# MLP first matrix on one Trainium2 core: PSUM banks of a pair laid out anew, first operands split during the output projection

## The chip, the cores and the metric

The kernel runs on one core of one Trainium2 chip. The metric is the time of one execution in microseconds (us) on the device; the engines are TensorE (PE, with its weight loads as PEld), VectorE (DVE), ScalarE (ACT), GpSimd (POOL) and SyncE (SP), whose queue issues the DMAs.

## The reference, cut to what matters

One decoder block over 1024 tokens of width 1024: a normed input projection, two mixers (a gated linear recurrence and sparse attention), a gated merge, an output projection with residual, and then the part that this case is about:

```python
h = h + merged @ w_out[l]
hn = rmsnorm(h, norm2_g[l])
h = h + jnp.square(jax.nn.relu(hn @ w_ff1[l])) @ w_ff2[l]
return rmsnorm(h, final_g)
```

Everything is float32. `w_ff1` is 1024 x 4096, `w_ff2` 4096 x 1024.

## The kernel before

Each float32 matrix product is made from three matmuls on operands that are split into a high and a low part (high x high, high x low, low x high). A split is one cast on ScalarE (high) and one subtraction on VectorE (low).

**The last stages.** The merge and the output projection run for two halves of the tokens (`th` 0 and 1, four tiles of 128 tokens each). The projection has, for each half of the columns (`dh`) and each tile `j`, 24 matmuls into a PSUM tile `po`, an addition on VectorE into the residual `hx` (L1375), and for the last half (`th` 1, `dh` 1) the second norm of tile `j` from the generator `norm2` (`next(n21)` twice): a square on ScalarE (L248), two small instructions on GpSimd (L249, L250), the scaled row on VectorE (`hn`, L1122), and then four sums and differences of the token blocks, on VectorE (L1134, L1136) and GpSimd (L1135, L1137).

**The first matrix of the MLP** is a Strassen-Winograd product: 7 products instead of 8 for each block of 256 output columns, called a pair here; there are `NP` = 16 pairs. `FORDER` is the order of the products in a pair: P1, P6, P7, P2, P5, P4, P3. Pairs 0 and 1 are interleaved at the start: P1 of both, P2 of both, then the rest of pair 0 and of pair 1. A product is 12 matmuls of 128x512 with stationary weights `w1op` and moving token blocks `xoh`, `xol`. The token blocks A11 and A12 are ready early; S1, S2, S3, S4 and A22 are made by `turn` after the first six products (`TURNS`): 16 transposes each through four PSUM tiles `pt`, each emptied by a cast (L1113) and a subtraction (L1114).

**Weights.** `f1_load` brings the two halves of a pair's weights (`w1r`); `f1_sums` makes the four weight differences T1 to T4 with four subtractions on GpSimd (L1174, tile `w1t`); `f1_prep` splits one product's weights into a slot of the ring `w1op` (five slots; cast L1185, subtraction L1186). P1, P2 and P3 take the raw blocks B11, B21, B22; the other products take T1 to T4. `ahead(s)` keeps the splits four steps ahead of the products (`AHEAD`). Before the first product the kernel calls `f1_sums(0)`, `f1_sums(1)` and `ahead(0)`; later pairs call `f1_sums(p + 1)` from `f1_prep`.

**PSUM.** There are two kinds of PSUM tiles: `psA`, two of them, each of two banks, and `psB`, four of them, each of one bank (also used by `po` and `pt`). A pair needs four banks: `a` takes P1 and then P2 on top, `c` takes P6, `d` takes P7 and then P4, `e` takes P5 and then P3. Before, `a` and `c` are the halves of one `psA` tile, and `d` and `e` are a `psB` tile each:

```python
pa = psA("f1a")
PB[p] = {"a": pa[:, :512], "c": pa[:, 512:], "d": psB("f1d"), "e": psB("f1e")}
```

After P1 ScalarE copies bank `a` to `p1` (L1225). After P6 VectorE adds `c` and `p1` to `u2` (L1217); after P7 it adds `d` and `u2` to `u3`; after P5 `e` and `u3`; after P4 `d` and `u2`; after P3 `e` and `u2`. Relu, square and the sums of the results follow on ScalarE, VectorE and GpSimd, and the results go to DRAM (`u_d`). The second matrix (`g_mm`, tiles `gA` of kind `psA` and `gB` of kind `psB`) reads them back.

The kernel is written with a tile framework, which puts in the semaphore waits and decides, from the order of the program and its own idea of what is ready, the order of instructions on each engine. So an engine's order in the trace is not always the program's.

Of the kernel before, what the change touches and what calls it, by code (L numbers as in the profile page):

```python
# [54 lines left out]
def tile_hybrid_block(ctx, tc, x, positions, norm1_g, w_in, lb_param, hgrn_norm_g, pe_k, pe_v,  # L55
# [15 lines left out]
    def psA(name="psA"):  # L71
        return ps.tile([128, 1024], F32, name=name, tag="A", bufs=2)

    def psB(name="psB"):
        return ps.tile([128, 512], F32, name=name, tag="B", bufs=4)
# [48 lines left out]
    class Stream:  # L124
# [5 lines left out]
        def add(self, srcs, shape):  # L130
            self.specs.append((srcs if isinstance(srcs, list) else [srcs], shape))
# [35 lines left out]
    def w_cols(w, c0, n, k0=0, k=KT):  # L167
        return w[k0 * 128:(k0 + k) * 128, c0:c0 + n].rearrange("(a p) c -> p a c", p=128)
# [420 lines left out]
    for t in range(NT):  # L589
        p = psB("pp")  # L590
# [557 lines left out]
    NP = FF // 256  # L1148
    FORDER = ("P1", "P6", "P7", "P2", "P5", "P4", "P3")
    FX = {"P1": "A11", "P2": "A12", "P3": "S4", "P4": "A22", "P5": "S1", "P6": "S2", "P7": "S3"}  # L1150
    FW = {"P1": "B11", "P2": "B21", "P3": "B22", "P4": "T4", "P5": "T1", "P6": "T2", "P7": "T3"}
    W1R, W1S, FOP, PB = {}, {}, {}, {}
# [4 lines left out]
    def ring(key, n, i, dt=F32):  # L1157
        r = RING.setdefault(key, {})
        if i % n not in r:
            r[i % n] = s4(dt, name=key)  # L1160
        return r[i % n]

    def f1_load(p):
        W1R[p] = []
        for q in range(2):
            r = ring("w1r", 4, 2 * p + q).rearrange("p (a c) -> p a c", a=4)
            nc.sync.dma_start(r, w_cols(w_ff1[0], p * 256, 256, k0=4 * q, k=4))
            W1R[p].append(r)

    def f1_sums(p):  # L1170
        b11, b12 = W1R[p][0][:, :, :128], W1R[p][0][:, :, 128:]
        b21, b22 = W1R[p][1][:, :, :128], W1R[p][1][:, :, 128:]
        ta, tb = [ring("w1t", 4, 2 * p + q).rearrange("p (x a c) -> p x a c", x=2, a=4) for q in range(2)]
        sub = lambda o, x_, y_: nc.gpsimd.tensor_tensor(o, x_, y_, op=OP.subtract)  # L1174
        sub(ta[:, 0], b12, b11)
        sub(ta[:, 1], b22, ta[:, 0])
        sub(tb[:, 0], b22, b12)
        sub(tb[:, 1], b21, ta[:, 1])
        W1S[p] = {"B11": b11, "B21": b21, "B22": b22, "T1": ta[:, 0], "T2": ta[:, 1], "T3": tb[:, 0],
                  "T4": tb[:, 1]}  # L1180

    def split2(src, op, shape):

        h, l = [op[:, x_ * 512:(x_ + 1) * 512].rearrange("p (a c) -> p a c", a=shape) for x_ in range(2)]
        nc.scalar.copy(h, src)  # L1185
        nc.vector.tensor_tensor(l, src, fb(h), op=OP.subtract)  # L1186
        return h, l
# [1 line left out]
    n_op = [0]  # L1189

    def f1_prep(p, nm):
        if nm == FORDER[4 if p == 1 else 3] and 0 < p < NP - 1:
            f1_sums(p + 1)
        FOP[p, nm] = split2(W1S[p][FW[nm]], ring("w1op", 5, n_op[0], F32R), 4)
        n_op[0] += 1
        if nm == FORDER[-1]:
            del W1S[p], W1R[p]
            if p + 2 < NP:
                f1_load(p + 2)
# [2 lines left out]

    def f1_prod(p, nm):
        if nm == "P1":
            pa = psA("f1a")
            PB[p] = {"a": pa[:, :512], "c": pa[:, 512:], "d": psB("f1d"), "e": psB("f1e")}
        bank = {"P1": "a", "P2": "a", "P6": "c", "P7": "d", "P4": "d", "P5": "e", "P3": "e"}[nm]
        dst, first = PB[p][bank], nm in ("P1", "P6", "P7", "P5")
        h, l = FOP.pop((p, nm))
        xh, xl = XO[FX[nm]]  # L1210
        for kt in range(4):
            for i, (w_, x_) in enumerate(((h, xh), (h, xl), (l, xh))):
                nc.tensor.matmul(dst, w_[:, kt, :], x_.kt(kt), start=first and kt == 0 and i == 0,  # L1213
                                 stop=kt == 3 and i == 2, skip_group_check=True)
        post = UP.setdefault(p, {})
        ps_ = PB[p]
        add = lambda o, a, b: nc.vector.tensor_tensor(o, a, b, op=OP.add)  # L1217

        def sq(o, eng):
            nc.scalar.activation(o, o, AF.Relu)  # L1220
            eng.tensor_tensor(o, o, o, op=OP.mult)

        if nm == "P1":
            post["p1"] = mlp.tile([128, 512], F32, name="p1", tag="p1", bufs=2)
            nc.scalar.copy(post["p1"], ps_["a"])  # L1225
        elif nm == "P6":
            post["u2"] = mlp.tile([128, 512], F32, name="u2", tag="u2", bufs=2)
            add(post["u2"], ps_["c"], post["p1"])
        elif nm == "P7":
            post["u3"] = mlp.tile([128, 512], F32, name="u3", tag="u3", bufs=2)  # L1230
            add(post["u3"], ps_["d"], post["u2"])
        elif nm == "P2":
            ua = post["ua"] = ring("ua", 2, p).rearrange("p (x c) -> p x c", x=2)
            nc.scalar.activation(ua[:, 0], ps_["a"], AF.Relu)
            nc.gpsimd.tensor_tensor(ua[:, 0], ua[:, 0], ua[:, 0], op=OP.mult)
        elif nm == "P5":
            ua = post["ua"]
            add(ua[:, 1], ps_["e"], post["u3"])
            sq(ua[:, 1], nc.vector)
            nc.sync.dma_start(u_d[p][0:2].rearrange("x p c -> p x c"), ua)  # L1240
        elif nm == "P4":
            ua = post["ua"]
            ut = post["ut"] = ring("ut", 2, p).rearrange("p (x c) -> p x c", x=2)
            ub = post["ub"] = ring("ub", 2, p).rearrange("p (x c) -> p x c", x=2)
            add(ut[:, 0], ps_["d"], post["u2"])
            sq(ut[:, 0], nc.vector)
            nc.gpsimd.tensor_tensor(ub[:, 0], ua[:, 0], ua[:, 1], op=OP.add)
            nc.gpsimd.tensor_tensor(ub[:, 1], ut[:, 0], ua[:, 1], op=OP.add)
            nc.sync.dma_start(u_d[p][2:4].rearrange("x p c -> p x c"), ub)
        else:  # L1250
            ua, ut = post["ua"], post["ut"]
            add(ut[:, 1], ps_["e"], post["u2"])
            sq(ut[:, 1], nc.gpsimd)
            uc = ring("uc", 1, 0)[:, (p % 2) * 512:(p % 2) * 512 + 512]
            nc.vector.tensor_tensor(ut[:, 0], ut[:, 0], ua[:, 0], op=OP.subtract)
            add(uc, ua[:, 0], ut[:, 1])
            nc.vector.tensor_tensor(ut[:, 1], ut[:, 1], ua[:, 1], op=OP.subtract)
            nc.sync.dma_start(u_d[p][4], uc)
            nc.sync.dma_start(u_d[p][5:7].rearrange("x p c -> p x c"), ut)
            del UP[p], PB[p]  # L1260
# [74 lines left out]
    def ahead(s):  # L1335
        while n_load[0] < min(len(seq), s + LOADS + 1):
            g_load(*seq[n_load[0]][1:])
            n_load[0] += 1
        while n_prep[0] < min(len(seq), s + AHEAD + 1):
            k, a, b = seq[n_prep[0]]  # L1340
            (f1_prep if k == "f" else g_prep)(a, b)
            n_prep[0] += 1

    g2b = load_row(norm2_g)
    for th in range(2):
        if th == 0:
            drain(zb.pop(0))
        else:
            for _ in merge(1, 0.0):
                pump(1300)  # L1350
        hs_ = []
        for j in range(4):
            t = th * 4 + j
            hx = s4(name="hx")
            nc.sync.dma_start(hx, x2[t * 128:(t + 1) * 128, :])
            hs_.append(hx)
        for dh in range(2):
            ws = [W.get() for _ in range(4)]
            if th == 1 and dh == 0:
                drain(n2)  # L1360
            if th == 1 and dh == 1:
                n21 = norm2(1, hs_)
                f1_load(0)
                f1_load(1)
            for j in range(4):
                p = psB("po")
                sl = slice(j * 128, (j + 1) * 128)
                for kt in range(KT):
                    w = ws[kt // 2]
                    mh, ml = M[th][kt // 4][0][:, kt % 4, sl], M[th][kt // 4][1][:, kt % 4, sl]  # L1370
                    mm3(p, (mh, ml), (w[0][:, kt % 2, :], w[1][:, kt % 2, :]), kt == 0, kt == KT - 1)
                    if kt == 3:
                        pump(2600)
                hv = hs_[j][:, dh * 512:(dh + 1) * 512]
                nc.vector.tensor_tensor(hv, hv, p, op=OP.add)  # L1375
                if th == 1 and dh == 1:
                    next(n21)
                    next(n21)
                pump(2600)
            del ws  # L1380
        del M[th]
        if th == 0:
            n2 = spawn(norm2(0, hs_))
        else:
            f1_sums(0)
            f1_sums(1)
            ahead(0)
            hs_ = None
    yb = None
# [4 lines left out]
    for s, (k, a, b) in enumerate(seq):  # L1394
# [6 lines left out]
        i, p = a, b  # L1401
# [48 lines left out]
```

## Time and profile before

| | |
|---|---|
| median of 3 runs | 1675.06 us (1674.51 to 1677.39) |
| profiled execution, its own time | 1676.41 us |
| span of the profile | 1674.6 us |
| PE busy | 1612.9 us (96%), 8342 matmuls |
| DVE, ACT, POOL busy | 1041.9 us (62%), 738.7 us (44%), 584.2 us (35%) |
| TensorE clock granted, mean | 0.988 |
| output projection, last matmul starts | 992.74 us |
| MLP first matrix, first and last matmul start | 1000.02 and 1361.44 us |

The span is the profiler's view from the first to the last instruction; the execution's own time is 1.8 us longer. Times in the rows are microseconds from the span's start. A matmul's row lasts 0.39 us in the trace, but matmuls are pipelined: the distance between starts is what one costs. In a timeline row a pair of square brackets holds the idle time before the instruction on its engine and what ended it.

### The profile page before, as it was taken

How to read it: one execution, taken by the hardware profiler on the slowest of the kernel's cores; microseconds unless marked ns; L12 is line 12 of the kernel's file. 1: busy time of each engine (PE TensorE's matmuls, PEld its weight loads, DVE VectorE, ACT ScalarE, POOL GpSimd, SP SyncE). 2: the span in 40 equal slices, each digit the busy share in tenths (PEclk: the TensorE clock that was granted, in tenths of full speed). 3: DMA queues.
4: the chain of work that ended last, by engine and by line, in shares of the span. 5: the costliest groups of instructions: out<-in, count | busy, mean ns of one | idle time of the engine just before them, and what ended most of it. 6: DMA issues, size and time to landing. Idle time of an engine off the chain costs nothing. (4 is left out here: it accounts for less than half of the span.)

```text
span 1674.6 us, 22913 instructions
## 1 busy us (share of the span) xinstructions
PE 1612.9 (96%) x8342; PEld 1346.1 (80%) x8342; DVE 1041.9 (62%) x1612; ACT 738.7 (44%) x1410; POOL 584.2 (35%) x583
## 2 busy tenths in 40 slices
PE   8999999999999999999999988999999999999998
PEld 7899887889887887788788767777777788888886
DVE  5463454123555568888874728666566686887765
ACT  5433333321664457777753314333333355334442
POOL 2121221110124263443412134555555321565552
PEclk9999999999999999999999998999999999999999
DMA  5210111232433000000075711443344489889853
GB/s 184 70 51 14 40 37 51 73 106 80 137 126 117 14 1 1 2 1 1 14 264 196 244 50 51 151 139 134 130 138 138 140 279 359 290 308 338 301 176 107
DMA packets 145395, 211.67 MB, mean 126 GB/s; under 512 B 11601, under 2 KB 72193, under 8 KB 145282
## 3 DMA queue, kind: packets, MB, share of 16 engines
q1 hardware_dynamic: 145282, 210.21, 37.4%
q8 instruction: 66, 1.08, 0.3%
q14 instruction: 47, 0.39, 0.1%
HBM read 164.03 MB, written 46.14 MB: 126 GB/s over the span
## 5 line engine op out<-in xcount | busy, mean ns | idle before, releaser
L1302 POOL TENSOR_TENSOR gr<-gw 128x512 f32<-128x512 f32 x80 | 125.7, 1583 | 133.7 <-DVE gu L1186 50.8
L1213 PE MATMUL f1a<-xoh,w1op 128*128 128x512 f32 x384 | 135.7, 417 | 33.2 <-ACT p L1225 24.2
L155 POOL TENSOR_TENSOR wlo<-wraw,whi 128x1024 fp32r<-128x1024 f32 (+1 forms) x28 | 67.4, 2408 | 274.8 <-ACT whi L152 270.4
L242 PE MATMUL gT<-xh,whi 128*128 128x512 f32 x384 | 152.7, 398 | 0.0
L244 PE MATMUL gT<-xh,wlo 128*128 128x512 f32 x384 | 150.3, 391 | 0.0
L243 PE MATMUL gT<-xl,whi 128*128 128x512 f32 x384 | 150.1, 391 | 0.0
L919 POOL TENSOR_SCALAR P<-P,den,gat 128x640 f32<-128x640 f32 (+7 forms) x128 | 99.6, 793 | 120.5 <-DVE den L915 61.4
L155 DVE TENSOR_TENSOR wlo<-wraw,whi 128x1024 fp32r<-128x1024 f32 (+2 forms) x59 | 80.8, 1377 | 94.5 <-ACT whi L152 89.8
L1186 DVE TENSOR_TENSOR gu<-gr,gu 128x512 fp32r<-128x512 f32 x112 | 101.5, 906 | 46.7 <-ACT gu L1185 46.5
L1185 ACT CAST gu<-gr 128x512 fp32r<-128x512 f32 x112 | 69.5, 620 | 133.5 <-DVE gx L1186 105.8
L1213 PEld LDWEIGHTS f1a<-xoh,w1op 128*128 128x128 f32 x384 | 77.2, 201 | 56.7 <-ACT p L1225 30.1
L937 DVE TENSOR_TENSOR pth<-pT,pth 128x512 fp32r<-128x512 f32 (+1 forms) x148 | 98.7, 682 | 21.3 <-ACT pth L936 19.9
L1186 DVE TENSOR_TENSOR gx<-gr,gx 128x512 fp32r<-128x512 f32 x112 | 109.2, 975 | 3.9 <-ACT gx L1185 3.8
L910 ACT ACTIVATE P<-sc,den 128x640 f32<-128x640 f32 (+7 forms) x128 | 89.6, 704 | 44.0 <-DVE den L901 39.2
L894 PE MATMUL sc<-kS,qS 128*128 128x512 f32 (+3 forms) x384 | 96.7, 361 | 0.6 <-ACT P L910 0.5
L1045 PE MATMUL oT<-pth,vS 128*128 128x512 f32 x264 | 96.5, 440 | 0.0
L936 ACT CAST pth<-pT 128x512 fp32r<-128x512 f32 (+1 forms) x148 | 84.9, 587 | 23.9 <-PE pT L934 21.6
L901 DVE TENSOR_REDUCE den<-sc 128x1 f32<-128x640 f32 (+7 forms) x96 | 84.5, 883 | 16.7 <-PE sc L897 16.1
L152 ACT CAST whi<-wraw 128x1024 fp32r<-128x1024 f32 (+2 forms) x87 | 88.5, 1038 | 12.8 <-PE po L243 6.1
L242 PE MATMUL gA<-gx,gu 128*128 128x512 f32 x224 | 87.3, 390 | 0.0
L243 PE MATMUL gA<-gx,gu 128*128 128x512 f32 x224 | 87.1, 389 | 0.0
L244 PE MATMUL gA<-gx,gu 128*128 128x512 f32 x224 | 87.1, 389 | 0.0
(332 smaller groups left out, 4430.1 us busy)
## 6 DMA issues: line engine op xcount, KB each, us to landing
gw<-in_w_ff_dram SPq DMA_DIRECT2D x160, 256.0 KB, 5.4
gr<-u_d SPq DMA_DIRECT2D x112, 256.0 KB, 5.1
wraw<-in_w_in_dram SPq DMA_DIRECT2D x40, 512.0 KB, 5.4
w1r<-in_w_ff_dram SPq DMA_DIRECT2D x32, 512.0 KB, 4.9
wraw<-in_w_out_dram SPq DMA_DIRECT2D x16, 512.0 KB, 7.8
u_d<-ua SPq DMA_DIRECT2D x16, 512.0 KB, 2.8
u_d<-ub SPq DMA_DIRECT2D x16, 512.0 KB, 2.8
u_d<-ut SPq DMA_DIRECT2D x16, 512.0 KB, 3.1
```

What stands on the lines that cost most here:

```text
L155: eng.tensor_tensor(lo, raw, fb(hi), op=OP.subtract)
L242: nc.tensor.matmul(o, l[0], r[0], start=start, stop=False)
L243: nc.tensor.matmul(o, l[0], r[1], start=False, stop=False)
L244: nc.tensor.matmul(o, l[1], r[0], start=False, stop=stop)
L894: nc.tensor.matmul(sc[:, cs], qS[th][g][:, hh, qsl], kS[half][br][:, g * 2 + x_, ks], start=x_ == 0, stop=x_ == 1 and not masks)
L910: nc.scalar.activation(PP[qb, g, i], sv[:, hh - h0], AF.Exp, bias=den[:, 2, i:i + 1], accum_out=den[:, 0, i:i + 1])
L919: nc.gpsimd.tensor_scalar(pv_, pv_, den[:, 1, i:i + 1], gat[:, qb, (g * 4 + h_) * 3 + 1 + br:(g * 4 + h_) * 3 + 2 + br], op0=OP.mult, op1= ...
L937: nc.vector.tensor_tensor(pth[:n, 1], pt[:n], fb(pth[:n, 0]), op=OP.subtract)
L1045: nc.tensor.matmul(oT, vv, pth[:m, x_], start=i == 0 and x_ == 0, stop=i == n - 1 and x_ == 1)
L1186: nc.vector.tensor_tensor(l, src, fb(h), op=OP.subtract)
L1213: nc.tensor.matmul(dst, w_[:, kt, :], x_.kt(kt), start=first and kt == 0 and i == 0, stop=kt == 3 and i == 2, skip_group_check=True)
L1302: nc.gpsimd.tensor_tensor(t0[:, 1], t1[:, 0], t1[:, 1], op=OP.add if GORDER[i][1][2] > 0 else OP.subtract)
```

## The change

Three edits. First, the four banks of a pair: `a` becomes a `psB` tile of its own, `c` and `e` become the two halves of one `psA` tile, `d` stays a `psB` tile. Second, `ahead(-1)` is called inside the output projection (`th` 1, `dh` 1, `j` 2, between the two steps of `norm2`): it splits the first four weight operands, P1 and P2 of pairs 0 and 1, which are raw blocks; for this `f1_load` fills `W1S[p]` with B11, B21 and B22. Third, `f1_sums(1)` is no longer called before the first product, but from `f1_prep` when P5 of pair 0 is prepared.

```diff
+        W1S[p] = {"B11": W1R[p][0][:, :, :128], "B21": W1R[p][1][:, :, :128], "B22": W1R[p][1][:, :, 128:]}
 
     def f1_sums(p):
-        b11, b12 = W1R[p][0][:, :, :128], W1R[p][0][:, :, 128:]
-        b21, b22 = W1R[p][1][:, :, :128], W1R[p][1][:, :, 128:]
+        b11, b21, b22 = [W1S[p][x_] for x_ in ("B11", "B21", "B22")]
+        b12 = W1R[p][0][:, :, 128:]
...
-        W1S[p] = {"B11": b11, "B21": b21, "B22": b22, "T1": ta[:, 0], "T2": ta[:, 1], "T3": tb[:, 0],
-                  "T4": tb[:, 1]}
+        W1S[p].update(T1=ta[:, 0], T2=ta[:, 1], T3=tb[:, 0], T4=tb[:, 1])
...
     def f1_prep(p, nm):
-        if nm == FORDER[4 if p == 1 else 3] and 0 < p < NP - 1:
+        if nm == FORDER[4 if p < 2 else 3] and p < NP - 1:
             f1_sums(p + 1)
...
         if nm == "P1":
-            pa = psA("f1a")
-            PB[p] = {"a": pa[:, :512], "c": pa[:, 512:], "d": psB("f1d"), "e": psB("f1e")}
+            pa = psA("f1c")
+            PB[p] = {"a": psB("f1a"), "c": pa[:, :512], "d": psB("f1d"), "e": pa[:, 512:]}
...
                 if th == 1 and dh == 1:
                     next(n21)
+                    if j == 2:
+                        ahead(-1)
                     next(n21)
...
             f1_sums(0)
-            f1_sums(1)
             ahead(0)
```

## Rows read from the trace of the kernel before

**Rows 1.** Waits of TensorE, whole span: waiter, releaser, total us, times, longest.
```profile
PE f1a L1213 <- ACT p L1225: 24.2, 14, 2.6
PE f1a L1213 <- DVE w1op L1186: 8.4, 1, 8.4
PE pt L1108 <- DVE hx L1375: 3.9, 1, 3.9
```

**Rows 2.** Three windows: start of the first matrix, its rest, the second matrix.
```profile
993.00:1050.20 57.20, 43.27 (x214) 35.35 (x212) 41.76 (x50) 23.82 (x44) 31.70 (x25) 0.85 0.17 59
1050.20:1361.80 311.60, 287.36 (x1214) 232.17 (x1213) 199.69 (x259) 109.40 (x187) 149.27 (x108) 0.97 0.43 148
1361.80:1674.60 312.80, 304.84 (x1345) 251.94 (x1343) 235.15 (x273) 127.92 (x225) 138.18 (x98) 0.99 0.77 270
```

**Rows 3.** Timeline of TensorE around pair 2: start, length, instruction.
```profile
1058.68 0.39 PE L1213 MATMUL f1a<-xoh,w1op 128*128 128x512 f32 x1
...
1061.40 0.39 PE L1213 MATMUL f1d<-xoh,w1op 128*128 128x512 f32 x1
...
1065.33 0.50 PE L1213 MATMUL f1a<-xoh,w1op 128*128 128x512 f32 x1 [2.63 <-ACT p L1225]
...
1069.76 0.62 PE L1213 MATMUL f1d<-xoh,w1op 128*128 128x512 f32 x2
...
1071.37 0.39 PE L1213 MATMUL f1a<-xoh,w1op 128*128 128x512 f32 x1
...
1074.09 0.39 PE L1213 MATMUL f1e<-xoh,w1op 128*128 128x512 f32 x1
```

**Rows 4.** Timeline of ScalarE, the copy of pair 2.
```profile
1064.70 0.58 ACT L1225 COPY p<-f1a 128x512 f32<-128x512 f32 x1
```

**Rows 5.** Timeline of VectorE in the same pair.
```profile
1066.60 0.69 DVE L1217 TENSOR_TENSOR uc<-ua,ut 128x512 f32<-128x512 f32 x1 [2.38 <-POOL ut L1221]
...
1067.81 0.68 DVE L1257 TENSOR_TENSOR ut<-ut,ua 128x512 f32<-128x512 f32 x1
```

**Rows 6.** Timelines of VectorE and of weight loads, last stage of the kernel.
```profile
1654.27 0.69 DVE L1314 TENSOR_TENSOR acc<-acc,gA 128x512 f32<-128x512 f32 x1 [4.25 <-PE gA L244]
...
1655.01 0.19 PEld L242 LDWEIGHTS gA<-gx,gu 128*128 128x128 f32 x1 [0.29 <-DVE acc L1314]
```

**Rows 7.** Timeline of SyncE's queue, first weights of the MLP.
```profile
947.43 3.16 SPq L1167 DMA_DIRECT2D w1r<-in_w_ff_dram  x4
```

**Rows 8.** Timeline of ScalarE, first splits.
```profile
999.37 2.16 ACT L1185 CAST w1op<-w1r 128x512 fp32r<-128x512 f32 x4
```

**Rows 9.** Timeline of VectorE, start of the first matrix.
```profile
997.60 0.68 DVE L1375 TENSOR_TENSOR hx<-hx,po 128x512 f32<-128x512 f32 x1
1004.88 2.27 DVE L1122 SCALAR_TENSOR_TENSOR hn<-hx,st,grow 128x1024 f32<-128x1024 f32 x1 [6.60 <-POOL st L250]
1007.19 1.63 DVE L1134 TENSOR_TENSOR hs<-hn 128x512 f32<-128x512 f32 x1
1008.74 3.43 DVE L1186 TENSOR_TENSOR w1op<-w1r,w1op 128x512 fp32r<-128x512 f32 x2
...
1016.26 0.68 DVE L1186 TENSOR_TENSOR w1op<-w1t,w1op 128x512 fp32r<-128x512 f32 x1
...
1029.03 0.69 DVE L1217 TENSOR_TENSOR u<-f1a,p 128x512 f32<-128x512 f32 x1 [0.57 <-PE f1a L1213]
```

**Rows 10.** Timeline of GpSimd, the same stretch.
```profile
998.99 2.51 POOL L1174 TENSOR_TENSOR w1t<-w1r 128x512 f32<-128x512 f32 x2
...
1011.59 1.72 POOL L1135 TENSOR_TENSOR hn<-hn 128x512 f32<-128x512 f32 x1
```

**Rows 11.** Timeline of TensorE, the same stretch.
```profile
992.97 1.47 PE L1108 MATMUL pt<-ident,hn 128*128 128x128 f32 x12
...
1010.54 1.22 PE L1213 MATMUL f1a<-xoh,w1op 128*128 128x512 f32 x2 [8.45 <-DVE w1op L1186]
...
1019.82 1.91 PE L1108 MATMUL pt<-ident,hn 128*128 128x128 f32 x16
```

## The prediction

> **What bounds the kernel now.** I read the page first: TensorE is busy 96% of the span and the granted clock is nearly full, so time can only come from stretches where TensorE waits, runs at its lower clock, or does less work. The change leaves the number of matmuls alone. So the next view was TensorE's waits over the whole span [rows 1]. The reader is to see that the first matrix (L1213) holds nearly all of them: 14 waits for the copy of P1 (ACT p, L1225), together 24.2 us, one of 8.4 us for a split of weights (DVE w1op), and one of 3.9 us just ahead of it. No wait of the second matrix is among them.
>
> The windows [rows 2] then tell how much each stage holds. One product of 12 matmuls takes 1074.09 - 1071.37 = 2.72 us when nothing disturbs it [rows 3]. From 1050.20, where P5 of pair 1 begins, to 1361.80 there are P5, P4 and P3 of pair 1 and 14 pairs of 7, which is 101 products or 274.7 us; the window has 311.6 us. The excess is 36.9 us: 24.2 us waits and 12.7 us of matmuls slowed by the clock (granted 0.97 of 2.4 GHz over the window, so short stretches at 1.2 GHz). From 993.00 to 1050.20 there are 11 products (29.9 us) and 80 transposes (5 groups of 16 at 1.91 us [rows 11], 9.6 us), 39.5 us of work in 57.2 us: an excess of 17.7 us, of which the two single waits of [rows 1] are 12.3 us. In the second matrix [rows 2] TensorE follows its loads without a gap that the change could reach; I expect it as long as before, 312.8 us, only earlier.
>
> **Part 1, the banks.** The timeline of pair 2 shows the wait in place [rows 3]. P1 runs from 1058.68 to 1061.40. TensorE then does half of P7 (bank `d`) and sits idle 2.63 us until 1065.33, when P6 starts into bank `c`. What released it is the copy of bank `a` [rows 4], from 1064.70 to 1065.28. P6 doesn't read `p1` and doesn't touch bank `a`; the two share only the two-bank tile. The end of the kernel shows the same pattern in another tile of that kind [rows 6]: VectorE reads the first half of `gA` at 1654.27, and the next weight load for `gA` waits for that read until 1655.01, though the matmuls behind it go to the other half. So I take it that the program puts a wait between a reader of one half and a writer of the other. After the idle time P6 takes 1069.76 - 1065.33 = 4.43 us in place of 2.72: after the gap TensorE runs part of it at the lower of its two clock levels (1.2 GHz in place of 2.4), so this wait of 2.63 us costs 4.3 us.
>
> In the new layout `a` is alone, so P6 has no reader to wait for. Two waits remain and have to be priced. P2 adds onto `a` and needs the copy: with P6, P7 in between it starts at 1058.68 + 3 x 2.72 = 1066.84, and the copy ended at 1065.28 [rows 4], 1.56 us before. And P5 is now the first writer of `e` beside `c`, so it will wait for VectorE's read of `c` (`u2`). It starts at 1058.68 + 4 x 2.72 = 1069.56. `u2` stands on VectorE behind `uc`, which waited 2.38 us for GpSimd, and behind L1257, which ends at 1068.49 [rows 5]; with 0.69 us of its own it ends at 1069.18, 0.38 us before P5. Both fit, the second barely, and pair 2 has the longest wait of all 14 (the mean is 24.2 / 14 = 1.73 us [rows 1]). Bounds: all 36.9 us come back, or some pairs keep half a microsecond, 14 x 0.5 = 7 us, so 30. I take 35, near the upper one, because the rows put both readers ahead of the writers.
>
> A rule speaks against this part. The Trainium skill, "Perfetto Trace Analysis", section "Optimizing Tensor Performance", says that independent groups should rotate through different PSUM banks, so that the emptying of one overlaps the matmuls of the next. By that rule the layout before is already right, since `a` and `c` are different banks, and a new one would bring nothing: 1665 us, the third rival below. The trace here does not bear it out as it stands: the banks differ and TensorE waits 24.2 us all the same.
>
> **Part 2, four splits earlier.** Removed from the start: four casts (2.16 us [rows 8]) and four subtractions on VectorE, the first two of which took 3.43 us [rows 9], 1.71 each, while GpSimd made its differences; alone one takes 0.68 us [rows 9]. They stood behind L1122 of tile 3, which waited 6.60 us for GpSimd, and that is the 8.45 us for which TensorE stood still until 1010.54 [rows 11]. Their data are there early: the four loads were issued from 947.43 [rows 7]. In the new place they run while TensorE still multiplies for tile 3. Behind them on ScalarE is only the square of tile 3, which waits for `hx` anyway. On VectorE they stand ahead of the rest of tile 2's norm and of the addition at 997.60 [rows 9]; the push is 0 if they fall into VectorE's idle times, 4 x 0.68 = 2.7 us if not, 4 x 1.71 = 6.8 us if GpSimd disturbs each. I take 2.7, as GpSimd has only two subtractions per tile there. SyncE's queue keeps its order; the loads of pairs 0 and 1 stay where they were.
>
> So TensorE can go from 993 straight into P1 and P2 of pairs 0 and 1 (10.9 us) and 16 transposes (1.9 us), at the full clock, until about 1006.
>
> **Part 3, the sums of pair 1 later.** GpSimd made eight differences from 998.99, and the rest of tile 3's norm (L1135) came behind all of them at 1011.59 [rows 10]. Four of them go; at up to 1.72 us, the length of that row, this is 6.9 us. L1135 then waits only for `hs`, which ended at 1007.19 + 1.63 = 1008.8 [rows 9]; with the push of 2.7 us that is 1011.5, no later than before, and without it 2.8 us earlier. The moved differences are wanted for P6 of pair 1, nine products later, and fit into GpSimd's idle time (31.70 busy of 57.2 [rows 2]); their cover gone, they would cost at most their 6.9 us.
>
> Together: S2 is complete after L1135 (1.7), L1136 (0.7), eight transposes (1.0) and a cast and a subtraction (0.6 and 0.7), so P6 of pair 0 starts at about 1011.5 + 4.7 = 1016.2. Before, its result was read at 1029.03, right after its end [rows 9], so it began at about 1026.3. The lead is 10 us. Two things can eat it: VectorE is already busy 41.76 of 57.2 us here [rows 2], and banks `a` of pairs 0 and 1 now take two of the four single-bank tiles through which the 80 transposes go (a missing tile cost 3.9 us once [rows 1]). Bounds: 4 (6 us given back) and 15 (almost the whole excess of 17.7). I take 10.
>
> **Sum.** The profiled execution took 1676.4 us, 1674.6 of span and 1.8 around it. 1676.4 - 35 - 10 = 1631.4. That execution is 1.35 us above the median, so I forecast 1630. The forecast's own range is 1675 - 52 = 1623 to 1675 - 34 = 1641.
>
> **The rivals.**
>
> *Part of the wait moves to P5 or P2.* For it: the slack of 0.38 us. Against: pair 2 is a bad pair. If half of wait and clock loss stays, 18 us come back in place of 35: 1647. Chance 0.13.
>
> *The early splits bring nothing.* The push on VectorE and the lack of `pt` tiles give all 10 us back: 1640. For it: VectorE's load; against: the 8.45 us gap had a cause that is gone. Chance 0.08.
>
> *The layout doesn't do what it says,* because the wait has another cause than the shared tile; only the start gains: 1665. [rows 6] speak against it. Chance 0.06.
>
> *Slower.* P5 waits for `u2` longer than P6 waited for the copy. Place: VectorE's queue, where `uc` waits for GpSimd. It decides from the point where the new wait and its lower clock (0.9 us a pair, 12.7 / 14) eat 45 us over 14 pairs, a wait of 2.3 us, so `u2` ending 2.7 us later than in [rows 5]. Two more differences of 1.72 us ahead of GpSimd's square would do it: 3.4 - 0.4 = 3.0 us of wait, 14 x 3.9 = 55 us, and 1630 + 55 = 1685. Nothing in [rows 5] shows such an order. Chance 0.03.
>
> **How the numbers follow.** The forecast has the remaining 0.70. The range 1620 to 1650 takes in its bounds, the second rival and the first, and leaves out the other two and the tails. A measurement here tells about 0.2%, 3.4 us. Faster: all but the last rival and a small part of unforeseen mixes, 0.95; same 0.02; slower 0.03.
>
> **What the profile after would show.** Part 1 is right if TensorE no longer waits for ACT p, and the stretch from P5 of pair 1 to the second matrix has about 276 us with a granted clock near 1.00; a row of L1213 waiting for DVE `u` would be the first rival. Parts 2 and 3 are right if the first matmul of the first matrix follows the output projection with no 8 us gap, and P6 of pair 0 starts some 23 us after the projection's last matmul in place of 33. The second matrix should keep its 313 us; if it grew, its loads would be the bound that I missed, and the prediction wrong there.

## The result and the profile after

The changed kernel takes 1646.42 us (median of four, 1646.09 to 1650.32) against 1676.22 us before: a ratio of 0.9828 with an interval of 0.9810 to 0.9847, 29.8 us or 1.7% less. The forecast was 45 us less. The profiled execution took 1650.32 us, the longest of the four; its part ahead of the changed place was 2.8 us longer than in the profile before (the projection's last matmul starts at 995.57 in place of 992.74), so stretches are counted from that matmul here.

The waits of TensorE over the whole span, which answer to [rows 1] (waiter, releaser, total us, times, longest; the lines in between belong to other stages):

```profile
PE f1c L1213 <- DVE u L1217: 9.2, 11, 0.9
PE pt L1108 <- DVE xol L1114: 5.6, 1, 5.6
...
PE f1a L1213 <- ACT p L1225: 1.7, 1, 1.7
```

The 24.2 us behind the copy and the 8.4 us behind the split are gone, but for one wait of 1.7 us for a copy and one of 1.6 us for a split, both in pair 0 at the start. Two new lines stand in their place. P5 (`f1c` is the two-bank tile now, P5 goes into its second half) waits for `u2` in 11 pairs, and a transpose waits once for VectorE.

The three windows that answer to [rows 2]: from the last projection matmul to the end of P7 of pair 1, from there to the second matrix, and the second matrix (stretch, its length, busy us of PE, PEld, DVE, ACT, POOL, clock, DMA share, GB/s):

```profile
995.80:1047.50 51.70, 42.68 (x213) 34.20 (x212) 38.60 (x50) 23.76 (x44) 29.88 (x25) 0.93 0.20 67
1047.50:1335.60 288.10, 278.95 (x1213) 225.89 (x1213) 190.95 (x259) 107.01 (x187) 147.33 (x108) 1.00 0.46 159
1335.60:1648.60 313.00, 305.00 (x1345) 252.07 (x1343) 234.11 (x273) 128.09 (x225) 137.71 (x98) 0.99 0.76 271
```

The second stretch went from 311.6 to 288.1 us, 23.5 less where 35 were forecast. The start, counted from the last projection matmul, went from 57.5 us (1050.20 - 992.74) to 51.9 us (1047.50 - 995.57), 5.5 less where 10 were forecast. The second matrix kept its 313 us. So both terms of the sum came short, each by about a third to a half.

**Where the second stretch loses.** One pair of the timeline, all engines in order of time (start, length, instruction, and in brackets the idle time before it and what ended it):

```profile
1087.38 1.57 SPq L1167 DMA_DIRECT2D w1r<-in_w_ff_dram  x2
...
1091.72 1.39 POOL L1175 TENSOR_TENSOR w1t<-w1r,w1t 128x512 f32<-128x512 f32 x1 [7.50 <-DMA w1r<-in_w_ff_dram]
...
1095.11 0.39 PE L1213 MATMUL f1a<-xoh,w1op 128*128 128x512 f32 x1
...
1098.83 1.29 POOL L1248 TENSOR_TENSOR ub<-ut,ua 128x512 f32<-128x512 f32 x1
...
1100.15 0.69 DVE L1255 TENSOR_TENSOR ut<-ut,ua 128x512 f32<-128x512 f32 x1 [3.54 <-POOL ub L1248]
...
1102.12 1.29 POOL L1175 TENSOR_TENSOR w1t<-w1r 128x512 f32<-128x512 f32 x1 [2.01 <-DVE w1op L1186]
...
1103.26 0.40 PE L1213 MATMUL f1a<-xoh,w1op 128*128 128x512 f32 x1
...
1103.38 1.04 POOL L1221 TENSOR_TENSOR ut<-ut 128x512 f32<-128x512 f32 x1
...
1104.45 0.69 DVE L1217 TENSOR_TENSOR uc<-ua,ut 128x512 f32<-128x512 f32 x1 [2.40 <-POOL ut L1221]
...
1106.26 0.68 DVE L1217 TENSOR_TENSOR u<-f1c,p 128x512 f32<-128x512 f32 x1
...
1106.86 0.68 DVE L1186 TENSOR_TENSOR w1op<-w1r,w1op 128x512 fp32r<-128x512 f32 x1
...
1107.00 0.50 PE L1213 MATMUL f1c<-xoh,w1op 128*128 128x512 f32 x1 [0.81 <-DVE u L1217]
```

P1 starts at 1095.11, P2 at 1103.26, and P5 could start at 1103.26 + 2.72 = 1105.98. It starts at 1107.00, because `u2` runs from 1106.26 to 1106.94. What it adds was ready 3.15 us before (P6 was done and the copy `p1` ended at 1103.11); `u2` stands in VectorE's queue behind two operations that waited for GpSimd, 3.54 us ahead of L1255 and 2.40 us ahead of `uc`. Read on around the circle: the split behind `u2` (1106.86) is the last reader of a weight buffer, its end at 1107.54 lets SyncE issue the next load at 1107.57, the load lets GpSimd begin its differences, behind them come `ub` and the square of `ut`, and these hold VectorE again. From load to load that is 1107.57 - 1087.38 = 20.19 us, and TensorE's seven products need 19.04.

This circle was there before too. The pair behind pair 2, in the trace of the kernel before:

```profile
1071.35 1.91 SPq L1167 DMA_DIRECT2D w1r<-in_w_ff_dram  x2
...
1084.68 0.69 DVE L1255 TENSOR_TENSOR ut<-ut,ua 128x512 f32<-128x512 f32 x1 [1.40 <-POOL ub L1248]
...
1086.01 0.63 ACT L1220 ACTIVATE ut<-ut 128x512 f32<-128x512 f32 x1 [3.11 <-DVE ut L1217]
...
1087.06 0.58 ACT L1225 COPY p<-f1a 128x512 f32<-128x512 f32 x1
...
1087.68 0.50 PE L1213 MATMUL f1a<-xoh,w1op 128*128 128x512 f32 x1 [1.42 <-ACT p L1225]
...
1090.82 0.69 DVE L1217 TENSOR_TENSOR u<-f1a,p 128x512 f32<-128x512 f32 x1
...
1092.13 1.89 SPq L1167 DMA_DIRECT2D w1r<-in_w_ff_dram  x2
```

From load to load this is 20.78 us. Of the eleven such distances between 1071.35 and 1307.58, eight are 20.75 to 20.89 us and three, each with a long wait of P6, 23.25 to 23.38. And the copy that P6 waited for hung on the same circle: the relu ahead of it on ScalarE (L1220) waited 3.11 us for VectorE, which had waited 1.40 us for GpSimd's `ub`. The new layout takes P6 out of the circle and leaves the rest, which sets the pace by way of P5.

**Where the start loses.**

```profile
995.99 0.50 PE L1213 MATMUL f1a<-xoh,w1op 128*128 128x512 f32 x1
...
996.38 1.28 DVE L1122 SCALAR_TENSOR_TENSOR hn<-hx,st,grow 128x1024 f32<-128x1024 f32 x1 [2.13 <-POOL st L250]
...
997.58 2.49 DVE L1186 TENSOR_TENSOR w1op<-w1r,w1op 128x512 fp32r<-128x512 f32 x4
...
1002.05 3.00 POOL L1175 TENSOR_TENSOR w1t<-w1r 128x512 f32<-128x512 f32 x2
...
1006.95 1.27 POOL L1175 TENSOR_TENSOR w1t<-w1r,w1t 128x512 f32<-128x512 f32 x1
...
1008.17 0.55 POOL L250 TENSOR_TENSOR st<-st,mhalf 128x1 f32<-128x1 f32 x1
1008.25 0.62 ACT L1185 CAST w1op<-w1t 128x512 fp32r<-128x512 f32 x1 [2.06 <-POOL w1t L1175]
...
1008.76 2.28 DVE L1122 SCALAR_TENSOR_TENSOR hn<-hx,st,grow 128x1024 f32<-128x1024 f32 x1 [1.94 <-POOL st L250]
1008.77 0.58 ACT L1113 CAST xoh<-pt 128x512 fp32r<-128x512 f32 x1
...
1012.17 0.68 DVE L1114 TENSOR_TENSOR xol<-pt,xoh 128x512 fp32r<-128x512 f32 x1
1012.32 1.27 POOL L1135 TENSOR_TENSOR hn<-hn 128x512 f32<-128x512 f32 x1 [2.36 <-DVE hs L1134]
...
1012.99 1.09 PE L1108 MATMUL pt<-ident,hn 128*128 128x128 f32 x4 [5.55 <-DVE xol L1114]
...
1014.30 1.05 PE L1213 MATMUL f1a<-xoh,w1op 128*128 128x512 f32 x2
...
1023.76 0.48 PE L1213 MATMUL f1c<-xoh,w1op 128*128 128x512 f32 x1
```

The first matmul follows the projection at once (995.99). After 28 of the 48 matmuls of P1 and P2 TensorE stands still for 5.55 us, since a subtraction on VectorE that empties a `pt` tile (1012.17) is queued behind L1122 of the last tile, L1122 waits for GpSimd's L250, and L250 ran behind three of the four weight differences. VectorE's queue is not all of it: the cast that this subtraction needs (L1113) ended only at 1009.35, as ScalarE's queue stood behind a split that waited 2.06 us for the same differences. The last 2.8 us, from 1009.35 to 1012.17, are VectorE's queue alone. The matmuls after the stop run first at the lower of the two clock levels (granted 0.50 from 1013.0 to 1016.4; a row of two lasts 1.05 us in place of 0.62), and P6 of pair 0 starts at 1023.76, 28.2 us after the last projection matmul: 33 before, 23 forecast.

### The profile page after: what moved, and what is told of

Read it like the earlier page. It is cut to its first block, busy times and chain, and to the rows that moved or that the text cites. A ratio compares the mean times of both kernels' runs of the same rounds, so it can differ in the third digit from the quotient of the medians.

```text
span 1648.6 us, 22914 instructions
## 1 busy us (share of the span) xinstructions
PE 1606.8 (97%) x8342; PEld 1341.0 (81%) x8342; DVE 1028.3 (62%) x1612; ACT 737.1 (45%) x1410; POOL 580.6 (35%) x583
## 5 line engine op out<-in xcount | busy, mean ns | idle before, releaser
L1213 PE MATMUL f1c<-xoh,w1op 128*128 128x512 f32 x384 | 127.7, 394 | 9.2 <-DVE u L1217 9.2
L1186 DVE TENSOR_TENSOR gu<-gr,gu 128x512 fp32r<-128x512 f32 x112 | 107.2, 958 | 45.3 <-ACT gu L1185 45.2
L1186 DVE TENSOR_TENSOR gx<-gr,gx 128x512 fp32r<-128x512 f32 x112 | 101.7, 908 | 4.6 <-ACT gx L1185 4.4
L1213 PEld LDWEIGHTS f1c<-xoh,w1op 128*128 128x128 f32 x384 | 72.0, 188 | 28.8 <-DVE u L1217 12.9
L1213 PE MATMUL f1a<-xoh,w1op 128*128 128x512 f32 x256 | 85.9, 397 | 3.4 <-ACT p L1225 1.7
L242 PE MATMUL gA<-gx,gu 128*128 128x512 f32 x224 | 87.3, 390 | 0.0
L244 PE MATMUL gA<-gx,gu 128*128 128x512 f32 x224 | 87.1, 389 | 0.0
```

The lines of the kernel that those rows point to most:

```text
L242: nc.tensor.matmul(o, l[0], r[0], start=start, stop=False)
L244: nc.tensor.matmul(o, l[1], r[0], start=False, stop=stop)
```

## The experiments

Start and stretch are measured as above; ratio and interval are against the kernel before on the same chip.

| run | start us | stretch us | median us | ratio (95%) |
|---|---|---|---|---|
| before | 57.5 | 311.6 | 1676 | |
| after | 51.9 | 288.1 | 1646.4 | 0.9828 (0.9810 to 0.9847) |
| e1 layout only | 60.0 | 287.8 | 1654.3 | 0.9874 (0.9859 to 0.9889) |
| e2 early splits, later sums only | 51.8 | 310.9 | 1668.6 | 0.9959 (0.9945 to 0.9973) |
| e3 `a` with `e` | 53.5 | 281.4 | 1641.1 | 0.9795 (0.9781 to 0.9810) |
| e4 old banks in pairs 0, 1 | 51.7 | 287.5 | 1646.7 | 0.9831 (0.9811 to 0.9851) |
| e5 tail on GpSimd | 52.2 | 313.4 | 1674.5 | 0.9989 (0.9980 to 0.9998) |
| e6 sums of pair 0 early | 47.6 | 287.6 | 1643.5 | 0.9802 (0.9786 to 0.9818) |
| e7 sums later | 52.2 | 287.6 | 1646.9 | 0.9824 (0.9809 to 0.9839) |
| e8 e3 and early start | 46.4 | 281.4 | 1634.0 | 0.9747 (0.9733 to 0.9762) |
| e9 two operations exchanged | 52.1 | 275.1 | 1634.4 | 0.9756 (0.9741 to 0.9770) |
| e10 e8 with the exchange | 47.4 | 282.5 | 1635.7 | 0.9760 (0.9744 to 0.9776) |
| e11 sums of pair 1 at the start | 56.7 | 288.0 | 1650.5 | 0.9853 (0.9837 to 0.9868) |
| e12 exchange and early start | 49.1 | 275.1 | 1630.9 | 0.9729 (0.9715 to 0.9742) |

**e1 and e2: the two halves of the change.** e1 is the kernel before with the two lines of the layout, e2 the kernel before with all but these.

```diff
-            pa = psA("f1a")
-            PB[p] = {"a": pa[:, :512], "c": pa[:, 512:], "d": psB("f1d"), "e": psB("f1e")}
+            pa = psA("f1c")
+            PB[p] = {"a": psB("f1a"), "c": pa[:, :512], "d": psB("f1d"), "e": pa[:, 512:]}
```

> Only the new layout of the banks, with the early splits and the later sums undone. Theory: the layout alone gives what the stretch from P5 of pair 1 to the second matrix lost, from 311.6 us before to about 288 us, and the waits of the first matrix for ACT p go, 11 or more short waits of P5 for DVE u come; the start keeps its 8 us wait for a split. 1676 - 23 = 1653 us, up to 5 us more if the two banks a of the first pairs hold up the transposes. Rival: the later sums, which move GpSimd's queue, are what removed the waits; then the 24 us of waits for ACT p stay here and the time stays within 4 us of before.

> Only the early splits and the later sums, with the banks as before. Theory: 14 waits for ACT p of about 24 us stay and the second stretch stays at about 311 us; at the start the 8.4 us wait goes, and with four free tiles for the transposes the 5.6 us wait for DVE xol does not come, so the start wins 8 to 11 us: 1666 us. Rival: the start wins no more than the 5.5 us that the whole change won there, because VectorE is the limit: 1671 us.

Waits of TensorE in e1, and in e2:

```profile
PE f1a L1213 <- DVE w1op L1186: 9.3, 1, 9.3
PE f1c L1213 <- DVE u L1217: 9.2, 11, 0.9
PE f1a L1213 <- ACT w1op L1185: 6.9, 1, 6.9
```

```profile
PE f1a L1213 <- ACT p L1225: 25.0, 15, 2.6
PE pt L1108 <- DVE xol L1114: 4.5, 2, 3.7
```

The layout alone removes every wait for the copy and brings the 11 waits for `u2`: the stretch is that of the full change. The other two edits leave the stretch as it was and bring the start to that of the full change. The gains of 21.6 and 7.3 us add up to 28.9 of 29.8, so there are two separate terms, and each was sized too high. In e2 the theory missed on the transposes: their waits for `xol` came with the old banks too (4.5 us in two), and the time lies between the theory's and the rival's. The layout costs something at the start, 60.0 us against 57.5, as long as the other two edits are out; with them in there is no such cost (51.9 against 51.8).

**e3 and e4: other banks.** e3 puts `a` and `e` into the two-bank tile and `c` alone; e4 keeps the old layout in pairs 0 and 1 only.

```diff
-            pa = psA("f1c")
-            PB[p] = {"a": psB("f1a"), "c": pa[:, :512], "d": psB("f1d"), "e": pa[:, 512:]}
+            pa = psA("f1a")
+            PB[p] = {"a": pa[:, :512], "c": psB("f1c"), "d": psB("f1d"), "e": pa[:, 512:]}
```

> The change, with bank e put beside a in the two-bank tile and c in a tile of its own. Theory (the wait is between a reader of one half and a writer of the other): P5, the first writer of e, follows P2 directly, and ScalarE's relu of a comes after P2, so each of about 14 pairs waits 1.0 to 1.5 us at P5 for ACT ua (L1234), and no longer for DVE u; with the lower clock after it 20 to 25 us in all against 13 now: 1652 to 1658 us. Rival (P5 waits for DVE u because of what VectorE does, whatever the tile): the waits for DVE u stay at about 9 us, none for ACT ua, and the time stays at 1646.

> The change, but pairs 0 and 1 keep the banks of before (a with c, d and e alone), so that all four single-bank tiles are free for the transposes at the start. Theory: the 5.6 us wait of the transposes for DVE xol at the start goes and nothing else changes: 1646 - 5 = 1641 us, 4 us either way. Rival: VectorE is the limit of the start, the wait comes back as another one of the same size: 1646 us.

My theory missed e3. P5 must now wait for the reader of P2's result in `a`, and I expected it to stand still. The timeline of TensorE shows another order:

```profile
1105.80 0.39 PE L1213 MATMUL f1a<-xoh,w1op 128*128 128x512 f32 x1
1106.29 0.50 PE L1213 MATMUL f1d<-xoh,w1op 128*128 128x512 f32 x1
...
1107.33 0.39 PE L1213 MATMUL f1d<-xol,w1op 128*128 128x512 f32 x1
1107.55 0.39 PE L1213 MATMUL f1a<-xoh,w1op 128*128 128x512 f32 x1
```

Between the last matmul of P2 (1105.80) and the first of P5 (1107.55, second half of `f1a`) the framework placed five matmuls of P4 into `d`. I take it that a wait which its own idea of times shows is filled with another product, while the wait for `u2` in the changed kernel was not filled; no run tests this. The switch isn't free: the gap at 1105.80 to 1106.29 is 0.49 us where 0.23 is usual. In e4 the transposes wait 4.5 us for VectorE in place of 5.6, and the time is the same. So the lack of single-bank tiles that the prediction named as an eater is not what holds the start.

**e5 and e7: two tries on the circle that failed.** e5 moves the three operations L1255 to L1257 from VectorE to GpSimd; e7 asks for the weight differences of the next pair when P3 is prepared, later than now.

```diff
-            nc.vector.tensor_tensor(ut[:, 0], ut[:, 0], ua[:, 0], op=OP.subtract)
-            add(uc, ua[:, 0], ut[:, 1])
-            nc.vector.tensor_tensor(ut[:, 1], ut[:, 1], ua[:, 1], op=OP.subtract)
+            nc.gpsimd.tensor_tensor(ut[:, 0], ut[:, 0], ua[:, 0], op=OP.subtract)
+            nc.gpsimd.tensor_tensor(uc, ua[:, 0], ut[:, 1], op=OP.add)
+            nc.gpsimd.tensor_tensor(ut[:, 1], ut[:, 1], ua[:, 1], op=OP.subtract)
```
```diff
-        if nm == FORDER[4 if p < 2 else 3] and p < NP - 1:
+        if nm == FORDER[4 if p < 2 else 6] and p < NP - 1:
```

> The change, with the three last operations of a pair (two subtractions into ut and the sum uc, L1255 to L1257) on GpSimd in place of VectorE, so that VectorE no longer stands still for GpSimd ahead of u2. Theory (P5 waits for u2 because u2 queues on VectorE behind these three): the 11 waits for DVE u of 9.2 us go, the stretch from P5 of pair 1 to the second matrix falls from 288 us to 275 to 280 us: 1634 to 1640 us. Rival: GpSimd, which loses up to 8 us of each pair waiting for weights, becomes the limit with three more operations of 1.3 us a pair, and TensorE waits for it by way of the copy of P1: 1646 us or more.

> The change, with f1_sums(p + 1) of pairs 2 and on called when P3 is prepared, three products later. Theory (GpSimd's queue, which waits 7 to 8 us for weights inside the sums, holds up ub and with it VectorE and u2): the waits of P5 for DVE u go or halve, 1646 - 5 to - 12 = 1634 to 1641 us, unless the splits of P6 now come too late (a wait of L1213 for w1op). Rival: the order on GpSimd is set by when data are there, not by where the call stands, and nothing moves: 1646 us.

The waits of e5 from 985 us on, which takes in the start and the stretch:

```profile
ACT w1op L1185 <- POOL w1t L1175: 56.8, 11, 9.3
...
PE f1c L1213 <- DVE ua L1217: 21.5, 8, 4.1
```

The 11 waits of P5 for `u2` are gone, as the theory said (though the slower pairs alone could have ended them), but the kernel is 28 us slower than the changed one: GpSimd is busy 226 us of 314 where it was busy 147 of 288, the weight differences come late, and TensorE waits up to 4.1 us for what hangs on them. In e7 nothing moves, the waits for `u2` are 9.2 us in 11 again: the differences were waiting for their load already (7.50 us in the rows above), so the place of the call made no difference, as the rival said.

**e6, e8, e11: the start.** e6 asks for the sums of pair 0 at the first quarter of the last projection tiles; e8 does so with the first splits too, in the layout of e3; e11 undoes the third edit.

```diff
                 if th == 1 and dh == 1:
+                    if j == 0:
+                        f1_sums(0)
                     next(n21)
...
-            f1_sums(0)
```

> The change, with f1_sums(0) called at the first tile of the output projection's last quarter, where GpSimd is idle, in place of after the last tile. Theory (at the start VectorE stands still for L250 of the last tile, which is behind these sums on GpSimd, and the transposes wait for VectorE): the 5.6 us wait for DVE xol falls below 2 us and the start gets 4 to 7 us shorter: 1640 us. Rival (the two banks a take the tiles that the transposes need): the wait stays, 1646 us; the run with the old banks in pairs 0 and 1, where it only split into 3.7 and 0.8 us, already speaks against it.

> The change with bank e beside a, and with f1_sums(0) and the four first splits both at the first tile of the output projection's last quarter. Theory: what the run with e beside a won in the second stretch (5 us) and what the start wins when neither VectorE nor GpSimd stands in front of the norm of the last tiles (6 to 10 us) add up: 1641 - 8 = 1633 us, 1630 to 1636. Rival: VectorE's own work is the limit of the start: 1639 to 1641 us.

> The changed kernel with the third edit alone undone: the weight sums of pair 1 are issued at the start again, behind those of pair 0. Theory (the order on GpSimd at the start is what holds the norm of the last tile, and with it VectorE and the transposes): four more sums of about 1 us stand ahead of it, the stretch up to P5 of pair 1 is 3 to 5 us longer than 52 us, and the time is about 1650 us. Rival (GpSimd works on what is ready first, so that the place in the program matters as little as it did for the later sums): the same time as the changed kernel, 1646 us.

With the differences of pair 0 out of the way of L250 the start is 4.3 us shorter (e6), with four more at this place it is 4.8 us longer (e11). So the place of the weight differences in GpSimd's queue moves the start. No run tells apart how much of it goes by way of the last tile's norm and how much by the casts on ScalarE that wait for the differences. In e6 a wait of 3.9 us of a transpose for VectorE is left, more than the 2 us I expected: L1122 still waits 2.31 us for L250 there, and the subtraction stands behind it. From e1 (60.0 us) over e11 (56.7) to the changed kernel (51.9) the two edits of the start can be told apart, with the new layout in place: the early splits bring 3.3 us, the later sums 4.8. e8 came out as the theory had it.

**e9, e10, e12: breaking the circle without loading GpSimd.** The square of the second half of `ut` goes to VectorE, and L1255 to GpSimd: one operation each way. VectorE then waits for GpSimd nowhere ahead of `u2`.

```diff
-            sq(ut[:, 1], nc.gpsimd)
+            sq(ut[:, 1], nc.vector)
...
-            nc.vector.tensor_tensor(ut[:, 0], ut[:, 0], ua[:, 0], op=OP.subtract)
+            nc.gpsimd.tensor_tensor(ut[:, 0], ut[:, 0], ua[:, 0], op=OP.subtract)
```

e10 adds this to e8. e12 adds to e9 the early sums and splits of e8, in the changed kernel's layout.

> The changed kernel with two operations of the first matrix's combination exchanged between engines: the square of the second half of ut goes from GpSimd to VectorE, and the subtraction of L1255 (ut less ua) goes from VectorE to GpSimd. VectorE then has no operation that waits for GpSimd ahead of u2, while GpSimd's load hardly changes. Theory (the 9.2 us in 11 waits of P5 for VectorE's u are VectorE's queue standing behind its waits for GpSimd, 3.5 us and 2.4 us a pair): these waits fall below 3 us, the stretch from P5 of pair 1 to the second matrix falls from 288 to about 279 us, and the time is about 1637 us. Rival (what holds u2 is ScalarE's copy and VectorE's own work, or the wait moves to GpSimd's longer subtraction as when the whole tail went there): no fewer waits, 1646 us or above.

> The kernel of the last batch that ran 1634 us (first combination's bank beside the last one, first sums and first splits at the first quarter) with the same exchange of two operations between VectorE and GpSimd. Theory: with that layout the order already fills the waits for u2, 2.0 us in 9 waits are left, so the exchange brings at most these: 1632 to 1634 us. Rival (GpSimd's subtraction is later than VectorE's was, and the sums on GpSimd stand behind it): above 1637 us.

> The changed kernel (its bank layout unchanged) with the two operations exchanged between VectorE and GpSimd, which alone ran 1634 us, and with the sums of pair 0 and the first splits both at the first quarter of the output projection's last tiles, which with the other layout brought 7 us. Theory (two separate terms: the queue behind GpSimd in every pair, and the work at the start): they add up, the stretch from the last projection matmul to P5 of pair 1 falls from 52 to 45 to 47 us, the one behind it stays at 275 us, and the time is 1627 to 1630 us, the fastest of all. Rival (the same wait is counted in both, as the kernel with the other layout, the early start and the exchange ran no faster than without the exchange): 1633 to 1635 us.

The second window of e9, and a pair of its timeline:

```profile
1045.50:1320.60 275.10, 274.98 (x1214) 227.75 (x1214) 245.84 (x259) 110.68 (x187) 170.04 (x108) 1.00 0.48 167
```

```profile
1094.18 1.75 POOL L1248 TENSOR_TENSOR ub<-ut,ua 128x512 f32<-128x512 f32 x1
1094.70 1.78 DVE L1221 TENSOR_TENSOR ut<-ut 128x512 f32<-128x512 f32 x1
...
1096.58 1.61 DVE L1217 TENSOR_TENSOR uc<-ua,ut 128x512 f32<-128x512 f32 x1
...
1100.41 0.68 DVE L1217 TENSOR_TENSOR u<-f1c,p 128x512 f32<-128x512 f32 x1
...
1102.91 0.39 PE L1213 MATMUL f1c<-xoh,w1op 128*128 128x512 f32 x1
```

`uc` no longer waits, `u2` ends at 1101.09, 1.8 us before P5 (1102.91), and no wait of TensorE for `u` is left. The stretch is 275.1 us, which is the 274.7 us of pure products that the prediction worked out. In e10 the exchange brings nothing, between the theory's 1632 to 1634 and the rival's 1637: in that layout the wait had been filled already, and what e8 has left is about 0.5 us a pair ((281.4 - 274.7) / 14), of the size of the switch to P4 and back; that this is all of it was not tested. e12 is the fastest version: 1630.89 us, a ratio of 0.9729 beside 0.9756 for e9. That is nearer to the theory's 1627 to 1630 us than to the rival's 1633 to 1635, though its start is 49.1 us and not 45 to 47.

## Why the prediction came out as it did

**The mechanism of part 1 was right.** Two halves of one PSUM tile wait for each other's readers, and with `a` alone the wait of P6 is gone: e1 shows it with the layout as its only edit. By the prediction's reading of the rule in the Trainium skill, "Perfetto Trace Analysis", section "Optimizing Tensor Performance", the layout would have brought nothing. e1's ratio of 0.9874, 21.6 us less, decides against this reading for this kernel: `a` and `c` had been different banks all along, and that was not enough.

**Part 1 was mis-sized: 23.5 us in place of 35.** The failed step is "`u2` ... ends at 1069.18, 0.38 us before P5. Both fit, the second barely". It held VectorE's times where pair 2 had them, counted from P1, and moved only TensorE forward to 19.04 us a pair, though the circle took 20.8 us or more from load to load in the same trace. In the shorter pair `u2` ends 1106.94 - 1095.11 = 11.83 us after P1's start where the forecast had 1069.18 - 1058.68 = 10.50, and P5 was due after 10.9. The circle through VectorE, SyncE's load and GpSimd takes 20.19 us, so 1.15 us a pair are lost, 11 x 1.15 = 12.7 of the 13.4 us that are left over 274.7. e9 takes VectorE's waits out of the circle and gets the 13 us back. The first rival, "part of the wait moves to P5", is what happened; its slack of 0.38 us was the right row to doubt, and 0.13 was too small a chance for it. That its 1647 us were met so closely is luck: it had 18 us from part 1 and 10 from the start, where 23.5 and 5.5 were measured. The forecast's own bounds, 30 to 36.9 us for part 1 and 1623 to 1641 us in all, were missed. The other slack, 1.56 us ahead of P2, was nearly used up too: the copy ended at 1103.11 and P2 started at 1103.26.

**Parts 2 and 3 were mis-sized: 5.5 us in place of 10.** Two steps failed. "TensorE can go from 993 straight into P1 and P2 of pairs 0 and 1 ... until about 1006" did not hold: it stops for 5.55 us after 28 of 48 matmuls. The forecast looked at L1135, behind GpSimd's differences, which indeed came earlier (16.8 us after the last projection matmul, 18.9 before); it left out L250 in the same queue, for which L1122 had waited 6.60 us [rows 9], and behind L1122 on VectorE the subtractions that free the `pt` tiles. And the splits did not run "while TensorE still multiplies for tile 3": on VectorE they stand behind L1122 of tile 2, at 997.58, 2 us after the last projection matmul, which is the wait of 1.6 us for a split. The addition into `hx` came no later for them (5.0 us after that matmul, 4.9 before). The step from L1135 to P6 took 11.4 us and not 4.7, because the rest of P1 and P2 was still to do. e6 and e11 move these differences and move the start by 4.3 and 4.8 us; in e4 the tiles are free and the start is as long. The 5.5 us lie within the bounds of 4 to 15.

**The rest.** The second matrix kept 313 us, and the second rival's "all 10 us back" did not come. The layout's own cost at the start (2.5 us in e1, without the early splits) was named but not priced by itself.

## What to carry to other kernels

When a stall of the bounding engine is removed, the other engines' waits don't shift with it: before trusting a slack read from the old trace, follow the queue behind the late operation once around, through loads and buffer releases, and compare the length of that circle with the new pace. Here the old trace had 20.8 us from load to load, the new one 20.2, and the pace would have been 19.0. Where an engine waits for a slower one ahead of urgent work, exchange operations so that the wait ends, and keep the slower engine's number of operations: one operation each way brought 12 us (GpSimd's busy time rose from 147 to 170 us and did no harm), three moved one way lost 28 us. At a stage's start count every operation in the slow engine's queue, the small ones too: a 0.55 us instruction behind weight sums held VectorE's queue, and by it part of a stop of TensorE of 5.55 us.

## What the runs showed of the hardware beyond expectation

A short stall was much cheaper than a long one. In the kernel before, the clock granted while P6 ran (2.8 us from its start) was 0.55 to 0.58 after the five waits of 2.31 to 2.63 us, and 1.00 after the nine of 0.60 to 1.54 us. The wait of 2.63 us cost 4.3 us, as the prediction had it [rows 3]; the next one, 1.42 us, left P6 at 2.87 us in place of 2.72. So the lower clock came with five of the 14 waits, and P6's slower matmuls make five times about 1.7 us, 8.6 of the 12.7 us that the prediction put down to the clock. After 0.81 us (the changed kernel's P5) the granted clock stayed at 1.00 and the wait cost 1.15 us. And VectorE had time to spare where its operations grew: in e9 the same 259 instructions took 245.84 us in place of 190.95, single ones 1.6 to 1.8 us in place of 0.68 while GpSimd's ran beside them (the rows of e9 above), and TensorE lost nothing by it.
